# Attention scores in an encoder trunk: the second pass of each head on 128 rows instead of 64, and keys and values in small rings

## The chip, the cores and the metric

The kernel runs on one core of a Trainium2 chip. The metric is the time of one execution on the device in microseconds, the median of several runs. The profile is of one execution; its times are counted from the first instruction.

Five engines work side by side, each through its own instructions in order: TensorE (PE in the profile, with its weight loads as PEld), VectorE (DVE), ScalarE (ACT), GpSimd (POOL) and SyncE (SP), whose queue here issues DMAs. POOL's queue issues others. A matmul needs its stationary operand loaded (LDWEIGHTS) before the moving operand streams through, and its result lands in a bank of PSUM.

## The reference

Two layers over a sequence of 2048 positions of width 1024. Layer 0 runs windowed attention (8 query heads on 2 key/value heads of 64, blocks of 128 positions, each block seeing itself and its two neighbours, with a sink logit), chunked spatial gating and a gate path; layer 1 is a convolution with gated linear scans in both directions. Each ends in a projection and a layer norm. The change touches only the scores of the attention:

```python
kb, vb = band(k), band(v)          # three neighbouring blocks of 128
s = jnp.einsum('bnqhgd,bnkhd->bnhgqk', qb, kb) * (HEAD_DIM ** -0.5)
s = jnp.where(valid, s, NEG_INF)   # |i - j| <= 128
m = jnp.maximum(s.max(-1, keepdims=True), sink_l)
p = jnp.exp(s - m)
o = einsum(p / (p.sum(-1) + exp(sink_l - m)), vb)
```

## The kernel before, in words

All of it is float32. Products that need more than TensorE's fast float32 form gives are made of pieces: a value is split into a high part, rounded to that form, and a low part, the rest, and a product is summed from several passes (`mm3`, lines 151 to 154, has three).

Layer 0 starts with the attention, block by block. For each pair of blocks `build` (line 299) loads x, transposes and modulates it, splits it and stores it. `project(blk)` (line 323) makes q, k and v of one block, rotates q and k on DVE, and prepares the keys: `ks` holds three 128-column pieces, the high part of key head 0 twice side by side, that of key head 1 likewise, and the low parts of both heads. Three transposes (L362) bring them to PSUM, and ACT copies them (L363) into `kT`, one tile for the whole sequence: 128 rows, 3 pieces, 2048 positions. In the first two pieces rows 0 to 63 and rows 64 to 127 hold the same high key part; in the third, rows 0 to 63 hold the low part of head 0 and rows 64 to 127 that of head 1. The values go to `vt`, also one tile for the whole sequence.

`scores(blk)` (line 370) splits q so that of a head's 128 rows one half is the high and the other the low part, transposes it into `qT`, and then makes the scores of each of the 8 heads in two passes into one PSUM bank (`psc`, three buffers):

```python
nc.tensor.matmul(ps[:, 0:W], lhsT=qt[:, h, :], rhs=kT[:, kv, k0:k0 + W], start=True, stop=False)
nc.tensor.matmul(ps[:, 0:W], lhsT=qt[r0:r0 + 64, h, :], rhs=kT[r0:r0 + 64, 2, k0:k0 + W], start=False, stop=True)
```

The first pass (L399) has 128 rows and gives high and low query times high key; the second (L400) has 64 rows and gives high query times low key. The width W is 384, and 256 for the first and the last block. DVE takes the scores out of PSUM with mask and minimum (L402), ACT takes the exponential (L405), DVE divides by the sum (L412). For blocks 0 to 13 DVE then transposes the probabilities in 32x32 squares into the tile `T` (L430; one buffer, two at the end), and 16 DMAs (L437), half of them on SP's queue and half on POOL's (from block 11 on all on SP's), put the squares in place, back into `P` (three buffers). Blocks 14 and 15 are transposed on TensorE (L422). `values(blk)` (line 441) multiplies with the values (L447).

The written order is a loop over blocks: scores of blk + 1, `build` for two blocks at every second, values of blk, projection of blk + 3. A planner, which simulates the program, moves instructions by priority as their inputs come; each engine then keeps the order that the planner gave. Behind the attention's last blocks TensorE already runs the first matmuls of the next stage (`sv_ps`, line 516).

Of the kernel before, what the change touches and what calls it, by code (L numbers as in the profile page):

```python
# [16 lines left out]
S = 2048  # L17
# [36 lines left out]
def kernel(  # L54
# [144 lines left out]
        else:  # L199
            tt(out=dst, in0=ps[pr, 0:w], in1=bias, op=ALU.add)  # L200

# [1 line left out]
    sa = ctx.enter_context(ExitStack())  # L203
    sb = ExitStack()
    ap = pool(sb, "attn", right)
# [83 lines left out]
    nc.gpsimd.affine_select(out=mask, in_=mask, pattern=[[-1, 384]], compare_op=ALU.is_ge, fill=-BIG,  # L289
                            base=256, channel_multiplier=1)  # L290

    kT = ap.tile([128, 3, S], F32R, name="kT")
    vt = ap.tile([128, S // 128, 128], F32, name="vt")
    NB = S // 128
    qkb = {}
    hTs = {}
# [26 lines left out]
    def project(blk):  # L323
        if blk >= NB:
            return
        hT = hTs[blk // 2]
        sl = slice(blk % 2 * 128, blk % 2 * 128 + 128)
        pk = bank(pj, "pj")
        for k in range(KD):
            mm3(pk[:, 0:256], hT[0][k][:, sl], hT[1][k][:, sl], wqh[:, k, 512:768], wql[:, k, 512:768], k == 0,  # L330
                k == KD - 1)
        pq = bank(pj, "pj")
        for k in range(KD):
            mm3(pq, hT[0][k][:, sl], hT[1][k][:, sl], wqh[:, k, 0:512], wql[:, k, 0:512], k == 0, k == KD - 1)
        qk = ap.tile([128, 10, 64], F32, tag="qk", bufs=4, name="qk")
        qkb[blk] = qk
        act(out=qk[:, 8:10, :], in_=pk[:, 0:128].rearrange("p (h d) -> p h d", h=2), func=AF.Copy)
        act(out=vt[:, blk, :], in_=pk[:, 128:256], func=AF.Copy)
        act(out=qk[:, 0:8, :], in_=pq.rearrange("p (h d) -> p h d", h=8), func=AF.Copy)
        rot = ap.tile([128, 4, 10, 8], F32, tag="rot", bufs=2, name="rot")  # L340
        for h0, h1 in ((8, 10), (0, 8)):
            n = h1 - h0
            cb = cos_t[:, blk:blk + 1, :].to_broadcast([128, n, 8])
            sb_ = sin_t[:, blk:blk + 1, :].to_broadcast([128, n, 8])
            t1 = qk[:, h0:h1, 0:8]
            t2 = qk[:, h0:h1, 8:16]
            r0, r1, r2, r3 = (rot[:, i, h0:h1, :] for i in range(4))
            tt(out=r0, in0=t1, in1=cb, op=ALU.mult)
            tt(out=r1, in0=t2, in1=sb_, op=ALU.mult)
            tt(out=r2, in0=t2, in1=cb, op=ALU.mult)  # L350
            tt(out=r3, in0=t1, in1=sb_, op=ALU.mult)
            tt(out=t1, in0=r0, in1=r1, op=ALU.subtract)
            tt(out=t2, in0=r2, in1=r3, op=ALU.add)
        ks = ap.tile([128, 3, 128], F32R, tag="ks", bufs=2, name="ks")
        kf = qk[:, 8:10, :]
        kd = ks[:, 0:2, :].rearrange("p k (u d) -> p k u d", u=2)
        act(out=kd, in_=kf[:, :, None, :].to_broadcast([128, 2, 2, 64]), func=AF.Copy)
        tt(out=ks[:, 2, :].rearrange("p (k d) -> p k d", k=2), in0=kf, in1=kd[:, :, 0, :].bitcast(F32),
           op=ALU.subtract)
        ps = bank(px, "px")  # L360
        for i in range(3):
            nc.tensor.transpose(ps[:, i * 128:i * 128 + 128].bitcast(F32R), ks[:, i, :], ident_r)  # L362
        act(out=kT[:, :, blk * 128:blk * 128 + 128], in_=ps[:, 0:384].rearrange("p (i n) -> p i n", i=3),  # L363
            func=AF.Copy)

    def window(blk):
        lo_b = max(blk - 1, 0)
# [2 lines left out]
    def scores(blk):  # L370
        if blk >= NB:
            return
        lo_b, nb = window(blk)
        W = nb * 128
        k0 = lo_b * 128
        m0 = (lo_b - blk + 1) * 128
        qk = qkb.pop(blk)
        qs = ap.tile([128, 8, 128], F32R, tag="qs", bufs=1, name="qs")
        qt = ap.tile([128, 8, 128], F32R, tag="qT", bufs=2, name="qT")
        nm = ap.tile([128, 8], F32, tag="nm", bufs=2, name="nm")  # L380
        rs = ap.tile([128, 8], F32, tag="rs", bufs=2, name="rs")
        es = ap.tile([128, 8], F32, tag="es", bufs=2, name="es")
        P = ap.tile([128, 8, 384], F32, tag="P", bufs=3, name="P")
        for kv in range(2):
            hs = slice(4 * kv, 4 * kv + 4)
            qv = qs[:, hs, :].rearrange("p h (u d) -> p h u d", u=2)
            split(qv[:, :, kv, :], qv[:, :, 1 - kv, :], qk[:, hs, :])
            ps = bank(px, "px")
            for i in range(4):
                nc.tensor.transpose(ps[:, i * 128:i * 128 + 128].bitcast(F32R), qs[:, 4 * kv + i, :], ident_r)  # L390
            act(out=qt[:, hs, :], in_=ps.rearrange("p (h n) -> p h n", h=4), func=AF.Copy)
        for kv in range(2):
            hs = slice(4 * kv, 4 * kv + 4)
            p = P[:, hs]
            r0 = 64 * kv
            for g in range(4):
                h = 4 * kv + g
                ps = bank(psc, "psc", (128, 384))
                nc.tensor.matmul(ps[:, 0:W], lhsT=qt[:, h, :], rhs=kT[:, kv, k0:k0 + W], start=True, stop=False)  # L399
                nc.tensor.matmul(ps[:, 0:W], lhsT=qt[r0:r0 + 64, h, :], rhs=kT[r0:r0 + 64, 2, k0:k0 + W],  # L400
                                 start=False, stop=True)
                nc.vector.tensor_tensor_reduce(  # L402
                    out=p[:, g, 0:W], in0=ps[:, 0:W], in1=mask[:, m0:m0 + W], scale=-0.125,
                    scalar=nsink[:, h:h + 1], op0=ALU.add, op1=ALU.min, accum_out=nm[:, h:h + 1])
                act(out=p[:, g, 0:W], in_=p[:, g, 0:W], func=AF.Exp, scale=-1.0, bias=nm[:, h:h + 1],  # L405
                    accum_out=rs[:, h:h + 1])
            tt(out=es[:, hs], in0=nm[:, hs], in1=nsink[:, hs], op=ALU.subtract)
            act(out=es[:, hs], in_=es[:, hs], func=AF.Exp)
            tt(out=rs[:, hs], in0=rs[:, hs], in1=es[:, hs], op=ALU.add)
            nc.vector.reciprocal(rs[:, hs], rs[:, hs])  # L410
            for g in range(4):
                ts(out=p[:, g, 0:W], in0=p[:, g, 0:W], scalar1=rs[:, 4 * kv + g:4 * kv + g + 1], scalar2=None,  # L412
                   op0=ALU.mult)
        nk = 4 * nb
        T = (tail[-1] if tail and blk % 2 else tq).tile([128, 12, 256], F32, tag="T", bufs=1, name="T")
        if blk >= PE_FROM:
            tv = T.rearrange("p j m -> p (j m)").rearrange("p (j v n) -> p j v n", j=3, v=2)
            for kv in range(2):
                for j in range(nb):
                    ps = bank(psc, "psc")  # L420
                    for g in range(4):
                        nc.tensor.transpose(ps[:, g * 128:g * 128 + 128], P[:, 4 * kv + g, j * 128:j * 128 + 128], ident)  # L422
                    if j % 2:
                        nc.vector.tensor_copy(tv[:, j, kv], ps)
                    else:
                        act(out=tv[:, j, kv], in_=ps, func=AF.Copy)
            Pb[blk] = tv
            return
        for kv in range(2):
            nc.vector.transpose(  # L430
                out=T[:, 0:nk, 128 * kv:128 * kv + 128].rearrange("p j (g q) -> p g j q", q=32),
                in_=P[:, 4 * kv:4 * kv + 4, 0:W].rearrange("p g (j q) -> p g j q", q=32))
        pv = P.rearrange("p h c -> p (h c)").rearrange("p (j i m) -> p j i m", j=3, i=4)
        for i in range(4):
            for r in range(4):
                dma = nc.sync if blk >= 11 or (i + r) % 2 == 0 else nc.gpsimd
                dma.dma_start(out=pv[32 * r:32 * r + 32, 0:nb, i],  # L437
                              in_=T[32 * i:32 * i + 32, 0:nk].rearrange("p (j r) m -> p r j m", r=4)[:, r])
        Pb[blk] = pv

    def values(blk):
# [2 lines left out]
        ops = bank(po, "po")  # L444
        for j in range(nb):
            for kv in range(2):
                nc.tensor.matmul(ops[64 * kv:64 * kv + 64, :], lhsT=vt[:, lo_b + j, 64 * kv:64 * kv + 64],  # L447
                                 rhs=pv[:, j, kv] if blk >= PE_FROM else pv[:, j, :, 128 * kv:128 * kv + 128],
                                 start=(j == 0), stop=(j == nb - 1))
        t, b = divmod(blk, 4)  # L450
# [72 lines left out]
    sb.close()  # L523


# [1 line left out]
    tp = pool(sp, "temp", left)  # L527
    pjb = pool(sp, "pjb", left, bufs=2, space=PSUM)
    pm = pool(sp, "pm", left, bufs=2, space=PSUM)
# [293 lines left out]
            vectors1()  # L823


# [1 line left out]
    sd.close()  # L827
    sp.close()
    turn = None
# [266 lines left out]

    se.close()

# [1 line left out]
    op = pool(ctx, "outp", right)  # L1100
    g_bc = op.tile([128, D], F32, name="g_bc1")
    b_bc = op.tile([128, D], F32, name="b_bc1")
# [74 lines left out]
```

## Time and profile before

| | |
|---|---|
| median of 3 runs | 1629.59 us (1624.6 to 1631.48) |
| span of the profiled execution, which is the only time that the profile gives for it | 1623.0 us |
| PE busy | 1525.7 us, 94% |
| DVE busy | 1243.6 us, 77% |
| ACT busy | 779.7 us, 48% |
| POOL busy | 517.0 us, 32% |
| score passes L399 and L400 | 128 each, from 67.7 to 372.1 us |
| key copies L363 | 16, from 60.2 to 314.3 us, 491 ns each |
| DMA | 366.72 MB, 226 GB/s in the mean |

Busy time is counted from start to modelled end, and matmuls overlap, so the distance from one matmul's start to the next start is what it costs PE. The time of a wait is put down to what ended last before the waiting instruction started; "issue" means that nothing the profile shows ended it.

### The profile page before, as it was taken

What the parts mean: (1) busy time and instruction counts of PE and PEld (TensorE: products, weight loads), DVE (VectorE), ACT (ScalarE), POOL (GpSimd) and SP (SyncE); (2) the same over time, 40 slices, a digit from 0 to 9 for tenths busy, and PEclk for the clock granted to TensorE, in tenths of its full rate; (3) what the DMA queues carried; (4) which work ended last, traced back from release to release, by engine and by line L of the source; (5) the groups of instructions that cost most, each with busy time, mean ns of one, the idle gap of its engine ahead of it and who ended that gap; (6) DMA issues with size and microseconds to landing.
All of it is one profiled execution on the core that took longest, in us unless ns stands there. A gap on an engine that the chain in (4) does not pass through costs nothing. (4 is left out here: it accounts for less than half of the span.)

```text
span 1623.0 us, 21775 instructions
## 1 busy us (share of the span) xinstructions
PE 1525.7 (94%) x7016; PEld 1193.3 (74%) x7016; DVE 1243.6 (77%) x2243; ACT 779.7 (48%) x1448; POOL 517.0 (32%) x703
## 2 busy tenths in 40 slices
PE   3999999999999999999999998999999899979997
PEld 3776666666787877887887776777787787867886
DVE  8478788765678667966776767879979989887795
ACT  3556666544332343243243307488478587771100
POOL 1022223202003200310120344867847765433121
PEclk9899999999999999999999998999999999999999
DMA  9356666765898989888785797787695757559652
GB/s 333 122 150 169 176 182 183 230 185 164 295 272 283 286 266 306 298 281 264 243 299 164 198 267 171 244 208 238 208 240 182 241 188 243 184 193 373 224 199 87
DMA packets 204602, 366.72 MB, mean 226 GB/s; under 512 B 54568, under 2 KB 100804, under 8 KB 204488
## 3 DMA queue, kind: packets, MB, share of 16 engines
q1 hardware_dynamic: 166632, 235.25, 46.8%
q0 software_dynamic: 37856, 130.08, 26.3%
q8 instruction: 56, 0.92, 0.2%
q14 instruction: 58, 0.48, 0.1%
HBM read 264.07 MB, written 79.68 MB: 212 GB/s over the span
## 5 line engine op out<-in xcount | busy, mean ns | idle before, releaser
L152 PE MATMUL pj<-ahi,hl 128*128 128x512 f32 x512 | 202.2, 398 | 10.1 <-DMA hl<-w_d 9.0
L148 ACT ACTIVATE hl<-raw 128x512 fp32r<-128x512 f32 x192 | 118.8, 628 | 192.5 <-DMA raw<-in_ev_w_in_dram 125.6
L153 PE MATMUL pj<-alo,hl 128*128 128x512 f32 x512 | 202.7, 396 | 0.0
L154 PE MATMUL pj<-ahi,hl 128*128 128x512 f32 x512 | 202.1, 396 | 0.0
L149 DVE TENSOR_TENSOR hl<-raw,hl 128x512 fp32r<-128x512 f32 x192 | 131.9, 695 | 66.8 <-ACT hl L148 66.4
L152 PEld LDWEIGHTS pj<-ahi,hl 128*128 128x128 f32 x512 | 97.6, 191 | 33.9 <-DMA hl<-w_d 11.3
L153 PEld LDWEIGHTS pj<-alo,hl 128*128 128x128 f32 x512 | 98.3, 192 | 20.6
L154 PEld LDWEIGHTS pj<-ahi,hl 128*128 128x128 f32 x512 | 97.9, 191 | 21.1
L402 DVE CUSTOM_DVE_ANT_0 P<-psc,mask,nsink 128x384 f32<-128x384 f32 (+1 forms) x128 | 75.6, 597 | 48.1 <-PE psc L400 45.6
L437 POOL DMA_DIRECT2D P<-T x88 | 48.3, 556 | 171.4 <-DMA xp<-in_x_dram 81.3
L853 POOL DMA_DIRECT2D hl<-w_d x128 | 71.0, 557 | 71.7 <-PE pj L154 59.5
L148 ACT ACTIVATE phl<-praw 128x512 fp32r<-128x512 f32 x56 | 35.4, 632 | 115.9 <-DMA praw<-in_od_w_in_dram 59.7
L499 POOL DMA_DIRECT2D ahi<-h_d x16 | 8.9, 558 | 255.5 <-PE px L154 146.6
L152 PE MATMUL pj<-wqh,hhi 128*128 128x256 f32 (+1 forms) x256 | 89.8, 354 | 0.0
L405 ACT ACTIVATE P<-P,nm 128x384 f32<-128x384 f32 (+1 forms) x128 | 76.4, 599 | 26.5 <-DVE nm L402 24.7
L153 PE MATMUL pj<-wql,hhi 128*128 128x256 f32 (+1 forms) x256 | 88.8, 347 | 0.0
L154 PE MATMUL pj<-wqh,hlo 128*128 128x512 f32 (+1 forms) x256 | 85.9, 349 | 0.0
L144 POOL TENSOR_SCALAR rstd<-mv 128x1 f32<-128x1 f32 x32 | 26.7, 834 | 185.8 <-DVE mv L588 160.4
L148 ACT ACTIVATE ahi<-yt 128x512 fp32r<-128x512 f32 (+1 forms) x44 | 32.4, 745 | 106.0 <-DVE yt L1073 67.9
L749 POOL TENSOR_TENSOR alo<-hm,ahi 128x512 fp32r<-128x512 f32 x32 | 47.9, 1498 | 94.7 <-issue 66.2
L919 DVE SCALAR_TENSOR_TENSOR xc<-X,vcol,xc 128x512 f32<-128x512 f32 (+2 forms) x96 | 77.2, 826 | 0.3
L152 PE MATMUL pm<-xhi,hg 128*128 128x512 f32 (+3 forms) x160 | 57.3, 370 | 19.9 <-ACT ra L938 13.2
(297 smaller groups left out, 4507.9 us busy)
## 6 DMA issues: line engine op xcount, KB each, us to landing
hl<-w_d POOLq DMA_DIRECT2D x128, 512.0 KB, 5.7
raw<-in_ev_w_in_dram SPq DMA_DIRECT2D x128, 256.0 KB, 4.0
w_d<-phl SPq DMA_DIRECT2D x40, 512.0 KB, 4.1
aw<-in_ada_w_dram SPq DMA_DIRECT2D x32, 512.0 KB, 5.9
hg<-w_d POOLq DMA_DIRECT2D x32, 512.0 KB, 4.8
P<-T SPq DMA_DIRECT2D x128, 96.0 KB, 3.7
aw<-in_ada_w_dram SPq DMA_DIRECT2D x8, 1024.0 KB, 8.3
xp<-in_x_dram SPq DMA_DIRECT2D x32, 256.0 KB, 3.5
```

What stands on the lines that cost most here:

```text
L144: nc.gpsimd.tensor_scalar(out=dst, in0=src, scalar1=mul, scalar2=EPS, op0=ALU.mult, op1=ALU.add)
L148: act(out=hi, in_=src, func=AF.Copy)
L149: tt(out=lo, in0=src, in1=hi.bitcast(F32), op=ALU.subtract)
L152: nc.tensor.matmul(ps, lhsT=ahi, rhs=bhi, start=first, stop=False)
L153: nc.tensor.matmul(ps, lhsT=ahi, rhs=blo, start=False, stop=False)
L154: nc.tensor.matmul(ps, lhsT=alo, rhs=bhi, start=False, stop=last)
L402: nc.vector.tensor_tensor_reduce(out=p[:, g, 0:W], in0=ps[:, 0:W], in1=mask[:, m0:m0 + W], scale=-0.125, scalar=nsink[:, h:h + 1], op0=ALU ...
L405: act(out=p[:, g, 0:W], in_=p[:, g, 0:W], func=AF.Exp, scale=-1.0, bias=nm[:, h:h + 1], accum_out=rs[:, h:h + 1])
L437: dma.dma_start(out=pv[32 * r:32 * r + 32, 0:nb, i], in_=T[32 * i:32 * i + 32, 0:nk].rearrange("p (j r) m -> p r j m", r=4)[:, r])
L749: nc.gpsimd.tensor_tensor(out=lo[:, j], in0=h, in1=hi[:, j].bitcast(F32), op=ALU.subtract)
L853: nc.gpsimd.dma_start(out=hl, in_=w_d[i])
L919: stt(out=xc[:, w], in0=xt[:, j0 + j:j0 + j + W], scalar=vcol1[:, 8 * j + g:8 * j + g + 1], in1=xc[:, w], op0=ALU.mult, op1=ALU.add)
```

## The change

The low key parts are stored like the high ones: for each key head twice, in rows 0 to 63 and in rows 64 to 127. `ks` and the key tile have four pieces instead of three. The second pass uses all 128 rows, so it gives high and low query times low key; its stationary operand is the same as that of the first pass.

The key tile for the whole sequence gives way to a ring of two buffers with room for six blocks each: four blocks of their own and one neighbour on each side. The key copy writes a block that is a neighbour of the next or the last group of four into both buffers (blocks 3, 4, 7, 8, 11 and 12). The values get a ring of seven tiles of one block each.

```diff
-    kT = ap.tile([128, 3, S], F32R, name="kT")
-    vt = ap.tile([128, S // 128, 128], F32, name="vt")
+    kTs = {}
+
+    def k_place(n, p):
+        if n not in kTs:
+            kTs[n] = ap.tile([128, 4, 768], F32R, tag="kT", bufs=2, name="kT")
+        return kTs[n][:, :, p * 128:p * 128 + 128]
+
+    vts = {}
...
-        act(out=vt[:, blk, :], in_=pk[:, 128:256], func=AF.Copy)
+        vt = ap.tile([128, 128], F32, tag="vt", bufs=7, name="vt")
+        vts[blk] = vt
+        act(out=vt, in_=pk[:, 128:256], func=AF.Copy)
...
-        ks = ap.tile([128, 3, 128], F32R, tag="ks", bufs=2, name="ks")
+        ks = ap.tile([128, 4, 128], F32R, tag="ks", bufs=2, name="ks")
...
-        tt(out=ks[:, 2, :].rearrange("p (k d) -> p k d", k=2), in0=kf, in1=kd[:, :, 0, :].bitcast(F32),
-           op=ALU.subtract)
+        tt(out=ks[:, 2:4, :].rearrange("p k (u d) -> p k u d", u=2),
+           in0=kf[:, :, None, :].to_broadcast([128, 2, 2, 64]), in1=kd.bitcast(F32), op=ALU.subtract)
         ps = bank(px, "px")
-        for i in range(3):
+        for i in range(4):
             nc.tensor.transpose(ps[:, i * 128:i * 128 + 128].bitcast(F32R), ks[:, i, :], ident_r)
-        act(out=kT[:, :, blk * 128:blk * 128 + 128], in_=ps[:, 0:384].rearrange("p (i n) -> p i n", i=3),
-            func=AF.Copy)
+        n, p = divmod(blk, 4)
+        places = [(n, p + 1)]
+        if p == 0 and n > 0:
+            places.insert(0, (n - 1, 5))
+        if p == 3 and blk < NB - 1:
+            places.append((n + 1, 0))
+        for place in places:
+            act(out=k_place(*place), in_=ps.rearrange("p (i n) -> p i n", i=4), func=AF.Copy)
...
-        k0 = lo_b * 128
+        kT = kTs[blk // 4]
+        k0 = (lo_b - 4 * (blk // 4) + 1) * 128
...
-                nc.tensor.matmul(ps[:, 0:W], lhsT=qt[r0:r0 + 64, h, :], rhs=kT[r0:r0 + 64, 2, k0:k0 + W],
-                                 start=False, stop=True)
+                nc.tensor.matmul(ps[:, 0:W], lhsT=qt[:, h, :], rhs=kT[:, 2 + kv, k0:k0 + W], start=False, stop=True)
...
-                nc.tensor.matmul(ops[64 * kv:64 * kv + 64, :], lhsT=vt[:, lo_b + j, 64 * kv:64 * kv + 64],
+                nc.tensor.matmul(ops[64 * kv:64 * kv + 64, :], lhsT=vts[lo_b + j][:, 64 * kv:64 * kv + 64],
```

More of the change, by code (lines that the diff above doesn't have):

```diff
@@ L394, in scores @@
             p = P[:, hs]
-            r0 = 64 * kv
             for g in range(4):
```

## The prediction

> **What bounds the kernel now.** The change touches only the attention of layer 0, so I first read the page for the whole and then that stage alone. The page's first part, and the stage's stretch from a table of stretches (busy time of each engine, then granted clock, DMA share, GB/s):
>
> ```profile
> span 1623.0 us, 21775 instructions
> PE 1525.7 (94%) x7016; PEld 1193.3 (74%) x7016; DVE 1243.6 (77%) x2243; ACT 779.7 (48%) x1448; POOL 517.0 (32%) x703
> ...
> 60.00:80.00 20.00, 20.00 (x112) 16.13 (x111) 6.91 (x37) 10.32 (x28) 0.00 (x0) 1.00 0.01 1
> 75.00:300.00 225.00, 224.54 (x1142) 153.38 (x1141) 177.90 (x591) 145.64 (x409) 55.83 (x98) 1.00 0.62 171
> ```
>
> PE is busy for 224.54 of 225 us at full clock; DVE is next with 177.90, which is 79%. A busy PE can still be badly used, so the waits of that stretch come next (who waited for whom: us in total, times, longest), PE's first and then the five largest of DVE:
>
> ```profile
> PE px L310 <- DMA xp<-in_x_dram: 0.4, 1, 0.4
> ...
> PEld psc L400 <- issue: 20.6, 92, 0.8
> ...
> DVE P L402 <- PE psc L400: 30.4, 26, 3.2
> DVE qs L149 <- ACT qs L148: 7.1, 6, 2.6
> DVE rs L409 <- ACT es L408: 2.6, 3, 1.2
> DVE ks L358 <- ACT ks L357: 1.9, 2, 1.4
> DVE hlo L149 <- ACT hhi L148: 1.9, 3, 0.9
> ```
>
> PE waits for nobody: it sets the pace, and DVE waits for the scores (30.4 us). But the weight load of the 64-row pass L400 sits 20.6 us in "issue", 92 times: something in PE's own stream is slow. The timeline of PE shows it; the first column is the start, and what a pass costs is the distance to the next start:
>
> ```profile
> 216.40 0.33 PE L399 MATMUL psc<-kT,qT 128*128 128x384 f32 x1
> 216.66 0.43 PE L400 MATMUL psc<-kT,qT 64*128 64x384 f32 x1
> 217.02 0.44 PE L399 MATMUL psc<-kT,qT 128*128 128x384 f32 x1
> 217.40 0.43 PE L400 MATMUL psc<-kT,qT 64*128 64x384 f32 x1
> 217.76 0.44 PE L399 MATMUL psc<-kT,qT 128*128 128x384 f32 x1
> 218.13 0.44 PE L400 MATMUL psc<-kT,qT 64*128 64x384 f32 x1
> 218.50 0.39 PE L154 MATMUL pj<-wqh,hlo 128*128 128x256 f32 x1
> 218.73 0.28 PE L152 MATMUL pj<-wqh,hhi 128*128 128x256 f32 x1
> 218.85 0.28 PE L153 MATMUL pj<-wql,hhi 128*128 128x256 f32 x1
> ...
> 219.54 0.39 PE L153 MATMUL pj<-wql,hhi 128*128 128x512 f32 x1
> 219.77 0.39 PE L154 MATMUL pj<-wqh,hlo 128*128 128x512 f32 x1
> ```
>
> Between 128-row matmuls the distance is 0.12 us for 256 columns (218.73 to 218.85) and 0.23 for 512 (219.54 to 219.77): 384 columns should take 0.175 us. Where a 128-row and a 64-row pass alternate, it is 0.36 to 0.38, and the 256-column matmul right behind (218.50) takes 0.23, not 0.12. Each change of the row count costs about 0.19 us.
>
> The Trainium skill (TensorEngine Tiling, Key Properties) says that a change of the tiling mode drains the engine; the trace agrees, with those 0.19 us. Another of its pages (TensorE: Matmul & The Clock Gate, LDWEIGHTS) says that a load's time does not hang on the row count, and by that alone a full-row pass would gain nothing; the pace of the rows above speaks for the drain.
>
> **The change, part by part.** The pace of a block today, from its key copy, of which blocks 2 and 14 are shown, and beside it the rows from which the added work is priced:
>
> ```profile
> 77.49 0.49 ACT L363 ACTIVATE kT<-px 128x384 fp32r<-128x384 f32 x1
> ...
> 308.34 0.49 ACT L363 ACTIVATE kT<-px 128x384 fp32r<-128x384 f32 x1 [1.30 <-PE px L362]
> ...
> L391 ACT ACTIVATE qT<-px 128x512 fp32r<-128x512 f32 x32 | 18.8, 595 | 17.6 <-PE px L390 17.4
> L149 DVE TENSOR_TENSOR qs<-qk,qs 128x256 fp32r<-128x256 f32 x32 | 12.5, 418 | 7.7 <-ACT qs L148 7.7
> L358 DVE TENSOR_TENSOR ks<-qk,ks x16: 277/290/293, 56.4 to 307.1; 128x128 fp32r<-128x128 f32 x16
> 211.91 0.37 PE L362 MATMUL px<-ident_r,ks 128*128 128x128 f32 x3
> 212.12 0.46 PE L152 MATMUL pj<-wqh,hhi 128*128 128x512 f32 x1
> ```
>
> Twelve blocks in 230.85 us: 19.24 us a block.
>
> *The second pass on 128 rows.* Six passes from 216.40 to 218.50 take 2.10 us, 0.70 for a head; at 0.175 a pass it is 0.35, and with the matmul behind a group of heads (0.11 each) I take 0.37 saved for a head. Eight heads in a block: 2.96 us. No 128-row pair of 384 columns stands in the trace, so the bounds are nothing saved (0.37 a pass stays) and 0.40 a head; I take 0.37, by the 256- and 512-column rows on either side.
>
> *Low keys stored twice.* L358 grows from 128x128 to 128x256: from 290 to the 418 ns of the qs row, 0.13 us a block on DVE, 2 us in all, and it stands two blocks ahead of its use. One transpose more for a block: three start in 0.21 us (211.91 to 212.12), so 0.07 us of PE.
>
> *The copies into the key ring.* L363 grows from 491 to the 595 ns of the qT row, and 6 of the 16 blocks (3, 4, 7, 8, 11, 12) write a second place: 16 x 0.10 + 6 x 0.60 = 5.2 us on ACT. ACT is busy 145.64 of 225 us, so at 19.24 us a block it has 6.8 us idle, and that covers a second copy with its 0.6. If that cover were gone, all 5.2 us would count.
>
> *The rings' new waits.* The first write into a reused key buffer (block 7 into that of blocks 0 to 3, block 11 likewise) waits on ACT's queue for the last score pass of block 3, or 7; behind it stand the exponentials L405, and for these wait DVE's sums and PE. In program order that last pass is two blocks ahead, some 34 us, so I take nothing. The bounds are nothing and one block of 19.24 us at each of the two places. A value tile comes round after seven blocks, and its last reader stands three blocks ahead: nothing. The buffers are not larger (a row of kT has 24,576 bytes as before, the values 3,584 where 8,192 were). No DMA is added or moved.
>
> **What is late next.** PE's need falls to 19.24 - 2.96 + 0.07 = 16.35 us a block. DVE: 177.90/225 x 19.24 = 15.21 busy, plus 0.13, plus its waits for ACT (7.1 + 2.6 + 1.9 + 1.9 = 13.5 us in the stretch, 1.15 a block), 16.5 if they all stay. The third is easily missed. The probabilities go through one buffer T: DVE transposes into it (L430), 16 DMAs read it out (L437, half on SP's queue), and only then can the next block's L430 write. For two blocks, DVE's transposes, SP's queue, and the median landing of these DMAs (last column):
>
> ```profile
> 239.74 3.42 DVE L430 STREAM_TRANSPOSE T<-P 128x1536 f32<-128x1536 f32 x2
> 259.05 3.43 DVE L430 STREAM_TRANSPOSE T<-P 128x1536 f32<-128x1536 f32 x2
> 277.67 3.43 DVE L430 STREAM_TRANSPOSE T<-P 128x1536 f32<-128x1536 f32 x2
> ...
> 245.84 0.37 SPq L304 DMA_DIRECT2D xp<-in_x_dram  x1
> 246.56 6.23 SPq L437 DMA_DIRECT2D P<-T  x8
> 262.51 7.88 SPq L437 DMA_DIRECT2D P<-T  x8
> ...
> P<-T SPq DMA_DIRECT2D x8, 96.0 KB, 5.8
> P<-T SPq DMA_DIRECT2D x8, 96.0 KB, 5.1
> ```
>
> For the later block, T is taken from 259.05 to 262.51 + 7.88 + 5.1 = 275.49, or 16.44 us, and the next L430 starts at 277.67. For the earlier one, SP's queue stood behind loads of x until 246.56, and T came free at 246.56 + 6.23 + 5.8 = 258.59, 18.85 us after its start, just before 259.05. So T alone asks for 17.65 us a block on average (estimate from two blocks). Part of the earlier block's delay are loads that wait for PE's transposes, and these come sooner with a faster PE; I take 0.35 off. The new pace is 17.3 us a block, bound by T and by DVE nearly together, and PE will wait about 1 us in each.
>
> **The sum.** Twelve blocks x (19.24 - 17.3) = 23.3. Ahead of 77.49 lie five heads in a stretch where DVE has only 6.91 of 20 us: 5 x 0.37 = 1.9. Behind 308.34 come 25 heads, 9.3 us at most. There each block waits in turn for the transposes and DMAs of the one two before, and PE for data (the gap at 316.44 below), so I take less than half, 4. In all 29 us, so a span of 1594 where the page has 1623.0. The median of the runs shown is 1629.59, their lowest 1624.6, so the profiled execution is a fast one; against the median the forecast is 1600. Nothing behind the attention is tied to absolute time and PE is at 94% over the whole, so I count the gain as kept.
>
> **The rivals.**
> (B) *PE stays the bound.* T and DVE keep up, all 128 heads count: 128 x 0.37 = 47, and 2 in the tail, 1580. For it: DVE's list of waits above has none for T's DMAs. Against: T's margin of 0.46 us (258.59 against 259.05) at today's pace.
> (C) *The shuffle holds.* If most blocks need the 18.85 us, 12 x 0.39 + 1.9 = 6.6 us, 1623; if half as bad, 1614. For it: SP's queue is in order and holds the loads of x. Against: the later block's 16.44.
> (D) *The full-row pass is no faster.* If the 0.37 comes from two passes into one bank and not from the row count, nothing is saved and the 16 transposes add 1.1: 1631. The Trainium skill's sentence on the load (TensorE: Matmul & The Clock Gate, LDWEIGHTS), named above, points this way. Against: the projection's passes share a bank at 0.23 for 512 columns.
> (E) *Slower, by the clock.* Today PE never waits, and its clock stays at 1.00. Where it did wait in the tail, it dropped:
>
> ```profile
> 316.44 1.19 PE L152 MATMUL pja<-hl,ahi 128*128 128x512 f32 x2 [1.39 <-DMA ahi<-h_d]
> 317.43 0.52 PE L399 MATMUL psc<-kT,qT 128*128 128x384 f32 x1
> ...
> 321.60 0.63 PE L152 MATMUL pja<-hl,ahi 128*128 128x512 f32 x1
> ```
>
> From 316.44 to 321.60 stand 6 passes of 0.23 and 2 heads of 0.73, 2.8 us at full clock, in 5.16: such a fall costs 2.3 us. If PE's new waits bunch into one gap of 1.4 us or more in each block, it decides from 29/2.3 = 13 falls on, one a block; two in each of 14 blocks would cost 64 and end at 1664. Against: 1 us of wait a block, in pieces. The Trainium skill (TensorE: Matmul & The Clock Gate, The HAM clock gate) asks for a whole idle window of about 3.4 us before the clock halves; the fall here came behind 1.39, so the trace is the stricter.
>
> **How the numbers follow.** My forecast (T and DVE pace, 1586 to 1614) 0.64; B 0.15; C 0.10; D 0.06; E 0.05. The range reaches from 1578 (B with the 0.40 bound) to 1616 (C's milder half): it leaves out the rest of C, D, E and a tail of B, about 0.2. A measurement here can tell about 0.5% from no change, so faster means below 1621.4. A, B and most of C: 0.88; D and the rest of C: 0.07; slower, E: 0.05.
>
> **What would show it.** L400 has 128 rows and starts 0.175 us behind L399, and its load's "issue" wait is gone; key copies 17.3 us apart; DVE's wait for psc well below 30.4, and new waits of PE for DVE or of L430 for P<-T's DMAs. Wrong if the passes still stand 0.37 apart, if the clock falls below 1.00 between 75 and 300 us, or if L363 waits for a score pass.

## The result, and the profile after

The changed kernel takes 1601.73 us in the median (1597.13 to 1601.9, four runs); the kernel before, run beside it, 1627.09 (1623.1 to 1631.48). The ratio is 0.984, with an interval of 0.982 to 0.986. A second series of the same kernel (e4_after below) gave 1597.85 us and 0.981 (0.977 to 0.984). The change makes the kernel faster by 25 to 29 us in the medians; 1600, or 29 us less, was forecast.

The page's first part after, and the same stretch of the attention as before (busy time of PE, PEld, DVE, ACT and POOL, then granted clock, DMA share, GB/s):

```profile
span 1600.0 us, 21817 instructions
PE 1481.9 (93%) x7032; PEld 1189.1 (74%) x7032; DVE 1241.8 (78%) x2243; ACT 780.8 (49%) x1454; POOL 514.5 (32%) x703
...
75.00:300.00 225.00, 216.13 (x1265) 170.54 (x1264) 197.55 (x660) 164.41 (x462) 62.85 (x108) 0.99 0.71 203
```

In the same 225 us PE now issues 1265 matmuls where it issued 1142, and it is no longer busy throughout: 224.54 became 216.13. DVE rose from 177.90 to 197.55, 88%. The timeline of PE shows why:

```profile
213.82 0.41 PE L413 MATMUL psc<-kT,qT 128*128 128x384 f32 x1
214.07 0.33 PE L414 MATMUL psc<-kT,qT 128*128 128x384 f32 x1
214.24 0.33 PE L413 MATMUL psc<-kT,qT 128*128 128x384 f32 x1
214.41 0.33 PE L414 MATMUL psc<-kT,qT 128*128 128x384 f32 x1
214.59 0.33 PE L413 MATMUL psc<-kT,qT 128*128 128x384 f32 x1
214.76 0.34 PE L414 MATMUL psc<-kT,qT 128*128 128x384 f32 x1
214.94 1.03 PE L316 MATMUL px<-ident,xp 128*128 128x128 f32 x8
```

From 214.07 to 214.94 stand five passes in 0.87 us, 0.174 each; before, a pass took 0.36 to 0.38. The weight loads show where the time was lost. Before, across a change of the row count, a load starts only when its own pass does (these two belong to the passes L400 at 216.66 and L399 at 217.02):

```profile
216.66 0.18 PEld L400 LDWEIGHTS psc<-kT,qT 64*128 64x128 f32 x1 [0.30 <-issue]
217.02 0.19 PEld L399 LDWEIGHTS psc<-kT,qT 128*128 128x128 f32 x1 [0.18 <-issue]
```

After, a load starts together with the pass ahead of its own (these two belong to the passes at 214.24 and 214.41), so its 0.19 us are hidden:

```profile
214.07 0.19 PEld L413 LDWEIGHTS psc<-kT,qT 128*128 128x128 f32 x1
214.24 0.19 PEld L414 LDWEIGHTS psc<-kT,qT 128*128 128x128 f32 x1
```

In the kernel before, all 128 loads of L400 start within 0.03 us of their own pass; after, those of L414 lead it by 0.17 us in the median. The 0.19 us that a change costs is as much as one load that isn't hidden. Whether PE empties itself at the change, or only takes its next load too late, these rows don't separate.

The waits of the stretch 75 to 300 us (who waited for whom: us in total, times, longest):

```profile
DVE P L415 <- PE psc L414: 13.3, 16, 2.2
...
ACT kT L378 <- PE px L370: 5.7, 6, 2.5
...
PE pj L154 <- DVE hlo L149: 3.7, 3, 2.2
...
PE px L316 <- DMA xp<-in_x_dram: 1.9, 2, 1.6
PE pja L152 <- DMA ahi<-h_d: 1.8, 1, 1.8
...
DVE T L443 <- DMA raw<-in_ev_w_in_dram: 0.9, 1, 0.9
...
PEld psc L414 <- issue: 0.8, 1, 0.8
```

The weight load of the second pass, which sat 20.6 us in "issue", has 0.8 left. DVE waits 13.3 us for scores instead of 30.4, and PE has waits of its own, some 9 us in all, for DVE, for x and for the next stage's data. The key copies of blocks 2 and 14 give the pace, and the first matmul of the gating stage (the tile `pjb`; count, shortest, median and longest ns, first and last start) marks the end of the attention:

```profile
75.08 0.59 ACT L378 ACTIVATE kT<-px 128x512 fp32r<-128x512 f32 x1
...
279.68 0.60 ACT L378 ACTIVATE kT<-px 128x512 fp32r<-128x512 f32 x1 [0.67 <-PE px L370]
```

```profile
L152 PE MATMUL pjb<-ahi,hl x128: 387/389/628, 348.1 to 827.5; 128*128 128x512 f32 x128
```

The same row of the kernel before:

```profile
L152 PE MATMUL pjb<-ahi,hl x128: 389/389/510, 379.1 to 857.3; 128*128 128x512 f32 x128
```

A block takes (279.68 - 75.08)/12 = 17.05 us instead of 19.24, and the attention ends 31.0 us sooner, at 348.1. The span fell by only 23.0. The remainder of the span, behind that first matmul, is 1243.9 us before and 1251.9 after. More on those 8 us in the point on the kept gain below.

### The profile page after: what moved, and what is told of

Its sections match the earlier page's. It is cut to its first block, busy times and chain, and to the rows that moved or that the text cites. A ratio compares the mean times of both kernels' runs of the same rounds, so it can differ in the third digit from the quotient of the medians.

```text
span 1600.0 us, 21817 instructions
## 1 busy us (share of the span) xinstructions
PE 1481.9 (93%) x7032; PEld 1189.1 (74%) x7032; DVE 1241.8 (78%) x2243; ACT 780.8 (49%) x1454; POOL 514.5 (32%) x703
## 5 line engine op out<-in xcount | busy, mean ns | idle before, releaser
L149 DVE TENSOR_TENSOR hl<-raw,hl 128x512 fp32r<-128x512 f32 x192 | 132.1, 697 | 70.4 <-ACT hl L148 70.0
L415 DVE CUSTOM_DVE_ANT_0 P<-psc,mask,nsink 128x384 f32<-128x384 f32 (+1 forms) x128 | 73.7, 596 | 20.6 <-PE psc L414 20.0
```

The lines of the kernel that those rows point to most:

```text
L149: tt(out=lo, in0=src, in1=hi.bitcast(F32), op=ALU.subtract)
L415: nc.vector.tensor_tensor_reduce(out=p[:, g, 0:W], in0=ps[:, 0:W], in1=mask[:, m0:m0 + W], scale=-0.125, scalar=nsink[:, h:h + 1], op0=ALU ...
```

## The experiments

The theory: a change of the row count costs PE about 0.19 us each time, and without these changes the pace is set by DVE and the buffer T nearly together. The rivals: the gain comes from the rings or from another order of the planner; or 64 rows are slow as such; or PE is still the bound.

For all runs, with pace by the key copies of blocks 2 to 14, end of the attention by the first `pjb` matmul, and the rest of the span:

| run | ratio to before (interval) | us a block | attention ends | rest |
|---|---|---|---|---|
| before; again (e5_before) | | 19.24; 19.27 | 379.1; 378.8 | 1243.9; 1247.6 |
| after; again (e4_after) | 0.984 (0.982 to 0.986); 0.981 (0.977 to 0.984) | 17.05; 17.18 | 348.1; 350.2 | 1251.9; 1248.4 |
| e1_ring: rings alone | 1.003 (1.001 to 1.005) | 19.36 | 379.3 | 1255.6 |
| e8_64rows: second pass back on 64 rows | 1.006 (1.004 to 1.009) | 19.51 | 379.6 | 1251.6 |
| e10_all64: both passes on 64 rows | 0.995 (0.993 to 0.998) | 18.18 | 361.6 | 1252.6 |
| e3_grouped | 1.000 (0.998 to 1.002) | 19.25 | 377.7 | 1253.5 |
| e6_forced | 1.004 (1.002 to 1.006) | 19.41 | 384.7 | 1245.8 |
| e7_nodiv | 0.997 (0.995 to 1.000) | 18.81 | 369.6 | 1252.8 |
| e9_xpool | 0.988 (0.986 to 0.990) | 16.64 | 352.5 | 1250.4 |
| e12_split | 0.982 (0.978 to 0.987) | 17.06 | 350.3 | 1244.8 |
| e13_both | 0.987 (0.984 to 0.990) | 16.62 | 354.0 | 1253.5 |
| e11b_xpool_mid | 0.986 (0.983 to 0.989) | 17.05 | 349.0 | 1250.0 |

**The rings without the full-row pass: e1_ring.** The changed kernel with three pieces of keys and the 64-row pass:

```diff
-            kTs[n] = ap.tile([128, 4, 768], F32R, tag="kT", bufs=2, name="kT")
+            kTs[n] = ap.tile([128, 3, 768], F32R, tag="kT", bufs=2, name="kT")
...
-        for i in range(4):
+        for i in range(3):
...
-                nc.tensor.matmul(ps[:, 0:W], lhsT=qt[:, h, :], rhs=kT[:, 2 + kv, k0:k0 + W], start=False, stop=True)
+                nc.tensor.matmul(ps[:, 0:W], lhsT=qt[r0:r0 + 64, h, :], rhs=kT[r0:r0 + 64, 2, k0:k0 + W],
+                                 start=False, stop=True)
```

> The rings alone: keys six blocks at a time and values in a ring of seven, but three key pieces and the 64-row second pass as before. If the gain comes from the row count (my theory), this kernel is as before, within 0.5%: passes 0.36 to 0.38 us apart, key copies 19.2 us apart, span about 1623 to 1626 us (6 copies of 0.49 us more on ACT, hidden). If the rings carry part of the gain (rival: other buffers let the planner start work earlier), key copies come below 18.5 us apart and the span below 1615. If the extra copies cost something, up to 3 us more.

It took 1632.41 us, and its attention ends where that of before does (379.3 against 379.1): the rings bring nothing there. Over the whole the kernel is even 5.4 us slower than the one before in the same series (1626.99), more than the 3 us allowed for; this lies behind the attention (see the last part of the point-by-point section).

**One line back: e8_64rows.** The changed kernel, with everything stored twice and copied twice as it is, and only the second pass on 64 rows again:

```diff
-                nc.tensor.matmul(ps[:, 0:W], lhsT=qt[:, h, :], rhs=kT[:, 2 + kv, k0:k0 + W], start=False, stop=True)
+                nc.tensor.matmul(ps[:, 0:W], lhsT=qt[64 * kv:64 * kv + 64, h, :], rhs=kT[64 * kv:64 * kv + 64, 2 + kv, k0:k0 + W], start=False, stop=True)
```

> The changed kernel with one line back: the second pass takes only the 64 rows of its key head, as before; tiles, rings, copies and the order of every engine's instructions are those of the changed kernel. If the row count carries the gain (theory), passes stand 0.37 us apart again, key copies about 19.2 us, attention over at 376 to 380 instead of 349, and the time is back at 1625 to 1632. If the planner's other order carries part of it (rival: the two kernels with reordered passes showed that order alone can cost 20 us), the time stays below 1615.

Its instructions stand on every engine in the same order as the changed kernel's, so the row count is the only difference. It took 1635.07 us (1624.68 for the kernel before in the same series), 33 us more than the first series of the changed kernel and 37 more than the second, and 3 more than the expected range. Its timeline of PE:

```profile
235.18 0.41 PE L413 MATMUL psc<-kT,qT 128*128 128x384 f32 x1
235.52 0.44 PE L414 MATMUL psc<-kT,qT 64*128 64x384 f32 x1
235.89 0.44 PE L413 MATMUL psc<-kT,qT 128*128 128x384 f32 x1
```

And its waits between 75 and 300 us:

```profile
DVE P L415 <- PE psc L414: 27.3, 26, 3.9
PEld psc L414 <- issue: 20.1, 93, 0.3
```

The distance of 0.34 to 0.37 is back, and the 20.1 us of "issue" with it; the attention ends at 379.6. So the whole gain hangs on the row count of this one line. The larger key copies and their second places are all in this kernel too, and its attention ends only 0.5 us later than that of before.

**64 rows, or the change of rows: e10_all64.** Both passes on the same 64 rows. The first pass leaves out the low query part, so less is computed; the written order of the instructions is again the changed kernel's.

```diff
-                nc.tensor.matmul(ps[:, 0:W], lhsT=qt[:, h, :], rhs=kT[:, kv, k0:k0 + W], start=True, stop=False)
-                nc.tensor.matmul(ps[:, 0:W], lhsT=qt[:, h, :], rhs=kT[:, 2 + kv, k0:k0 + W], start=False, stop=True)
+                nc.tensor.matmul(ps[:, 0:W], lhsT=qt[64 * kv:64 * kv + 64, h, :], rhs=kT[64 * kv:64 * kv + 64, kv, k0:k0 + W], start=True, stop=False)
+                nc.tensor.matmul(ps[:, 0:W], lhsT=qt[64 * kv:64 * kv + 64, h, :], rhs=kT[64 * kv:64 * kv + 64, 2 + kv, k0:k0 + W], start=False, stop=True)
```

> The changed kernel with both passes on the same 64 rows (the first pass leaves out the low part of the query, so that term is missing), in the same order of instructions. If the change of the row count is what costs (theory), a pass behind a pass takes 0.175 us though it has 64 rows, and only the ends of a run of passes cost, about 0.09 us in front and 0.11 behind: a head between projections about 0.55 us, in a run of heads 0.35; attention over at 355 to 362 and the time 1604 to 1612. If a 64-row pass is slow by itself (rival), each takes 0.36 and the time is as with the 64-row second pass or worse, 1625 or more.

The timeline of PE in this run:

```profile
137.07 0.39 PE L154 MATMUL pj<-wqh,hlo 128*128 128x512 f32 x1
137.39 0.45 PE L413 MATMUL psc<-kT,qT 64*128 64x384 f32 x2
137.67 0.34 PE L414 MATMUL psc<-kT,qT 64*128 64x384 f32 x2
137.85 0.33 PE L413 MATMUL psc<-kT,qT 64*128 64x384 f32 x1
138.02 0.34 PE L414 MATMUL psc<-kT,qT 64*128 64x384 f32 x1
138.29 0.39 PE L152 MATMUL pj<-wqh,hhi 128*128 128x256 f32 x1
138.51 0.28 PE L153 MATMUL pj<-wql,hhi 128*128 128x256 f32 x1
...
224.15 0.44 PE L413 MATMUL psc<-kT,qT 64*128 64x384 f32 x1
224.43 0.33 PE L414 MATMUL psc<-kT,qT 64*128 64x384 f32 x1
224.61 0.33 PE L413 MATMUL psc<-kT,qT 64*128 64x384 f32 x1
...
225.13 0.34 PE L414 MATMUL psc<-kT,qT 64*128 64x384 f32 x1
225.39 0.88 PE L316 MATMUL px<-ident,xp 128*128 128x128 f32 x6
```

Between two 64-row passes the distance is 0.17 to 0.18 us, the same as between two 128-row passes. So 64 rows aren't slow; the change is, going in and coming out, and its price falls half on the matmul ahead of it and half on the one behind. Going in, the projection at 137.07 takes 0.32 instead of 0.23, and the first passes behind it 0.28 instead of 0.17 (132.36 to 132.53 in the changed kernel). Coming out, the last pass takes 0.27 (138.02 to 138.29) and the projection behind it 0.22 instead of 0.12. Behind transposes the first pass proves less: it takes 0.28 here (224.15 to 224.43), but 0.25 in the changed kernel too (213.82 to 214.07), where the row count doesn't change. Before, every 64-row pass had a change on both of its sides; here only a group's two ends have one. The time follows: 1616.0 us, 19 less than e8_64rows, where the changed kernel is 33 to 37 below it. The attention ends within the expected range, the time lies 4 us above it.

One thing besides the change of rows is in this run. The two passes at 137.39 start 0.006 us apart, and so do, within 0.01 us, the two at 137.67: they are the last head of one key head, on rows 0 to 63, and the first of the other, on rows 64 to 127, side by side. This happens in 7 of the 16 blocks and saves some 0.35 us each time (an estimate, two passes of 0.175), 2.5 us in all, so it does not carry the result. The Trainium skill (TensorE: Matmul & The Clock Gate, Why this matters for your kernels) says that a single matmul over few rows takes the time of one over 128, and the distances of 0.17 to 0.18 agree. It also says that a change of the tiling mode drains the engine (TensorEngine Tiling, Key Properties), and the two ends of a group agree, as they would with a load that comes too late.

**The same saving in the kernel before: e3_grouped and e6_forced.** The passes of two heads in the order 128, 128, 64, 64, which halves the changes of row count without any other storage. First in program order only:

```diff
+                if g % 2 == 0:
+                    for j in (h, h + 1):
+                        pss[j] = bank(psc, "psc", (128, 384))
+                        nc.tensor.matmul(pss[j][:, 0:W], lhsT=qt[:, j, :], rhs=kT[:, kv, k0:k0 + W], start=True,
+                                         stop=False)
+                    for j in (h, h + 1):
+                        nc.tensor.matmul(pss[j][:, 0:W], lhsT=qt[r0:r0 + 64, j, :],
+                                         rhs=kT[r0:r0 + 64, 2, k0:k0 + W], start=False, stop=True)
```

> The kernel before, with its three key pieces and whole-sequence tiles, but the passes of two heads are ordered 128, 128, 64, 64 rows: half as many changes of the row count, the same matmuls. If each change costs about 0.19 us (theory), the second of two like passes starts 0.175 us behind the first, a pair of heads takes about 1.08 us instead of 1.46, and 8 heads save 1.5 us a block: key copies about 17.8 us apart, span about 1623 - 15 = 1608. If a 64-row pass is slow by itself (rival), 64 follows 64 at 0.36 and the gain is at most half of that, span 1616 or more; if two passes into one bank were the cost, both kinds fall to 0.175, 1 a block would be left of the gain, and the first rows of the timeline show it. DVE may get its scores two at a time and give some of it back.

The planner put most passes back in turns, so nothing changed (ratio 1.000). e6_forced adds an ordering edge from the second 128-row pass to the first 64-row one, and then the groups stay:

```diff
+                        if j == h:
+                            tc.add_manual_dep(m2.ins, m1.ins.name,
+                                              mybir.DependencyInfo(mybir.DependencyClass.NoSync,
+                                                                   mybir.DependencyReason.DATA),
+                                              reason="pass order")
```

> The kernel before with the passes of two heads bound to the order 128, 128, 64, 64 rows (in the run before, the planner had mostly put them back into turns). Where two like passes did stand together, the second of them cost 0.175 to 0.18 us and the change between them 0.26 to 0.37. If the change of the row count is the cost (theory), a pair of heads takes 1.0 us instead of 1.46, 8 heads save 1.8 us a block, key copies 17.4 to 17.8 us apart, attention over at about 357 and the span about 1603 to 1608. If the 64-row pass itself is slow (rival), 64 behind 64 takes 0.36 and half of the gain is missing, span 1615 or more. If it lies in the pair of passes into one bank, each pass into another bank than the last takes 0.175 and all four do, attention over near 350.

The passes became cheap where grouped. The timeline of PE in e6_forced:

```profile
216.44 0.51 PE L402 MATMUL psc<-kT,qT 128*128 128x384 f32 x2
216.88 0.61 PE L405 MATMUL psc<-kT,qT 64*128 64x384 f32 x2
217.42 0.44 PE L402 MATMUL psc<-kT,qT 128*128 128x384 f32 x1
```

That is 0.98 us for two heads instead of 1.4. Yet the kernel took 1631.77 us. In the planner's new order PE runs into waits that before did not have, and around some of them the clock fell. The stretch of the attention and a short one inside it, and PE's timeline at the same place:

```profile
75.00:300.00 225.00, 215.44 (x1131) 153.51 (x1131) 171.88 (x591) 144.88 (x407) 56.01 (x98) 0.95 0.61 170
...
200.00:203.00 3.00, 3.00 (x10) 1.30 (x11) 2.77 (x6) 2.11 (x6) 0.00 (x0) 0.50 0.92 311
```

```profile
197.32 1.94 PE L310 MATMUL px<-ident,xp 128*128 128x128 f32 x8 [2.82 <-ACT hhi L148]
...
202.02 4.89 PE L458 MATMUL po<-P,vt 128*64 128x512 f32 x12
```

PE waits 2.82 us for ACT's split, from 194.50 to 197.32, and from 196 us on, in the middle of the wait, the granted clock is 0.50: the twelve value matmuls take 4.89 us where they take 2.79 at full clock. Only from 207 us on is it 1.00 again. This is rival E of the prediction, in another kernel. Over the 225 us PE stood idle for 9.6 us (0.5 before), and its clock was 0.95 in the mean; the changed kernel's is 0.99. The idle time and 0.05 of 225 us for the clock make up to some 20 us (an estimate), about as much as the order was expected to save, 1.8 us a block.

**What bounds the new pace: e7_nodiv.** The changed kernel without the division by the sum (L425), 8 x 0.42 us less on DVE in each block; the output is left unnormalised.

```diff
-            for g in range(4):
-                ts(out=p[:, g, 0:W], in0=p[:, g, 0:W], scalar1=rs[:, 4 * kv + g:4 * kv + g + 1], scalar2=None,
-                   op0=ALU.mult)
```

> The changed kernel without the division by the sum (left out: 8 x 0.42 us of DVE for each block, so the output is not normalised). After the change key copies are 17.05 us apart where PE's stream needs about 16.35. If DVE is what holds PE up (theory), DVE falls from 15.2 to 11.8 us a block and key copies come 16.4 us apart: attention over at about 340 instead of 349, time 8 us lower. If the shuffle buffer T is the hold (rival), it stays within 2 us of the changed kernel. If PE alone is the bound, likewise nothing.

It was not faster than the changed kernel but 19 us slower, at 1620.92. DVE's busy time in the stretch fell to 148.76 us, but in the planned order loads of x stand on SP's queue behind the shuffle's transfers (eight transfers from 148.69 to 157.11, loads of x at 157.21), and PE waited for them (waits of e7_nodiv, 75 to 300 us):

```profile
PE px L316 <- DMA xp<-in_x_dram: 18.6, 5, 5.3
```

The clock was 0.95 in the mean of the stretch. So this run does not tell DVE from T. It shows that another planned order can cost some 20 us here although work is saved.

**The loads of x off SP's queue: e9_xpool.** From the third pair of blocks on, POOL's queue issues them:

```diff
+            ld = load if u < 2 else nc.gpsimd.dma_start
```

> The changed kernel with the loads of x from the third pair of blocks on issued by POOL's queue and not by SP's, where they and the 8 shuffle DMAs of a block wait for each other in order. If that queue costs PE its last microsecond a block (theory), key copies come 16.5 us apart and the time falls by up to 6 us, to about 1594. If PE's waits come from DVE and ACT (rival), the time stays within 2 us of 1600, or rises where the planner's order changes.

The key copies of blocks 2 and 14 now stand (274.88 - 75.15)/12 = 16.64 us a block apart, near PE's own need of 16.35. Yet the kernel took 1605.31 us, and the attention ends at 352.5, later than the changed kernel's. The 16.64 hangs on its last copy alone. Block 13's key copy, in this run and then in the changed kernel:

```profile
261.50 0.60 ACT L379 ACTIVATE kT<-px 128x512 fp32r<-128x512 f32 x1 [0.35 <-PE px L371]
```

```profile
261.42 0.60 ACT L378 ACTIVATE kT<-px 128x512 fp32r<-128x512 f32 x1
```

Up to there both kernels need 16.94 us a block; then block 14's keys come 4.8 us sooner here, and block 15's do not (285.95 against 285.52). So the loads' new queue did not make the front faster; one block's projection moved ahead. The rear of the pipeline, the value products L460 (L461 here) of blocks 1 and 9, stand at 113.61 and 251.26 in the changed kernel, 17.2 us a block, and at 114.39 and 250.66 in this one, 17.0; at block 10 the rear is behind (276.82 against 273.27). From 280 to 350 us ACT and DVE then wait for T's transfers:

```profile
ACT T L440 <- DMA P<-T: 8.8, 1, 8.8
...
DVE T L438 <- DMA P<-T: 6.5, 1, 6.5
DVE T L444 <- DMA P<-T: 4.9, 1, 4.9
```

The changed kernel has the same three waits there, with 7.7, 5.9 and 1.5 us.

**The tail: e12_split, e13_both, e11b_xpool_mid.** From block 11 on, all 16 transfers of a shuffle are issued by SP. In the changed kernel these issues take 11.67 and 10.61 us for the last two blocks. e12_split gives half of them back to POOL for these two; e13_both does the same on top of e9_xpool.

```diff
-                dma = nc.sync if blk >= 11 or (i + r) % 2 == 0 else nc.gpsimd
+                dma = nc.sync if blk == 11 or (i + r) % 2 == 0 else nc.gpsimd
```

> The changed kernel with the value-shuffle transfers of blocks 12 and 13 issued again from two queues, SP and POOL; only block 11 keeps all sixteen on SP. Theory: the end of the attention is set by the chain through tile T, and sixteen issues on SP take 10.6 us there against some 8 us with two queues, so each of two blocks saves about 2.5 us: the last score stretch (block-14 key copy to first pjb matmul) falls from 68.4 to about 64 us, the time to about 1597 us, pace of the blocks unchanged at 17.1. Rival: the tail is set by the projection work and PE, not by T; then the stretch stays within 1 us of 68.4 and the time within 2 us of the changed kernel's.

> The kernel of e9_xpool (x loads of blocks 2 on issued by POOL) with the same split of the shuffle transfers of blocks 12 and 13. Theory: the steady pace stays at 16.6 us a block, and the tail, 77.6 us in e9_xpool with DVE waiting 4.9 us and ACT 8.8 us for T, loses about 5 us: attention ends near 347 us, time about 1600 us. Rival: what e9_xpool lost in its tail comes from PE reaching the tail earlier and T's chain being as long anyhow; then the tail stays above 75 us and the time at about 1605 us.

SP's queue in e12_split, for these two blocks, and DVE's transposes ahead of the second:

```profile
295.27 7.28 SPq L450 DMA_DIRECT2D P<-T  x8
315.90 7.95 SPq L450 DMA_DIRECT2D P<-T  x8
```

```profile
312.39 3.44 DVE L443 STREAM_TRANSPOSE T<-P 128x1536 f32<-128x1536 f32 x2 [0.18 <-issue]
```

The issues are shorter as expected, but the second block's transposes stand at 312.39 where the changed kernel has them at 309.18 (310.87 in e4_after). There they had waited 1.52 us for T's transfers. Here no such wait stands before them; instead DVE had just done three splits of the gating stage's data (L149 at 309.79 and 310.91, behind waits of 1.49 and 0.43 us for ACT). So what was saved on the queue did not bring the transposes forward. The tail from the key copy of block 14 is 350.3 - 279.25 = 71.0 us, longer than 68.4 (69.6 in e4_after), and the time is 1598.86 us, between the two series of the changed kernel. The theory of the queue's issue time fell; so did its half in e13_both, with a tail of 354.0 - 275.29 = 78.7 us and 1607.32 us. For e11b_xpool_mid only the pairs 2 to 5 load x by POOL:

```diff
-            ld = load if u < 2 else nc.gpsimd.dma_start
+            ld = nc.gpsimd.dma_start if 1 < u < 6 else load
```

> The changed kernel with the x loads of the middle four builds (u from 2 to 5, blocks 4 to 11) issued by POOL, and those of the last two again by SP; the shuffle transfers as in the changed kernel. Theory: what e9_xpool and e13_both lost behind the key copy of block 14 (77.6 and 78.7 us where the changed kernel took 68.4) came from the late x loads in POOL's queue, so here the early blocks keep the pace of 16.6 us, the tail returns to about 69 us, the attention ends near 343 us and the time is about 1594 us. Rival: PE, DVE and T have a fixed amount of work up to the end of the attention, and a faster start only makes the tail wait; then the attention ends at 348 to 352 us as in all of these variants and the time stays between 1598 and 1606 us.

The attention ended at 349.0 us and the time was 1603.24, as the rival had it. But the key copies came 17.05 us apart, so the faster start that both expected outcomes took for granted did not come about, and the run does not show what one would have been worth. With the second pass on 128 rows the attention ends between 348.1 and 354.0 us in all of these kernels, except e7_nodiv. None of them measurably beats the changed kernel.

## Why the prediction was right, point by point

**The cost of a change of rows: right.** Predicted 0.19 us a change and 0.175 a pass; measured 0.174 a pass, and in e10_all64 about 0.2 a change. Not in the forecast was that a group's first pass behind transposes takes 0.25 in the changed kernel. Rival D (no faster) is excluded by the changed kernel's own rows, two passes into one bank at 0.174, and by e8_64rows; e10_all64 shows that what counts is the change, not the rows.

**The new pace: right in size, with luck in it.** Predicted 17.3 us a block with PE waiting about 1 us in each; measured 17.05 and 17.18, and PE's non-busy time is (225 - 216.13)/225 x 17.05 = 0.67 us a block. PE's own work is then 16.38, where 16.35 was predicted. But the 17.3 was worked out from T, and this half is not borne out: in the stretch the transposes L443 stood waiting for 1.3 us in all, and no wait for the transfers P<-T is among them. Such waits come in the tail, 280 to 350 us: 1.5 us in the changed kernel, 2.1 in e4_after, 4.9 in e9_xpool. DVE, the other half, is busy 197.55 of 225 us, 88%; PE waits 3.7 us for its splits, but 1.9 for x and 1.8 for the next stage's data as well. What sets the 17.05 was not separated, since e7_nodiv ran into x loads. Rival B (PE alone, 16.35 us a block) was reached by no run, as the 16.64 of e9_xpool comes from one copy; rival C, with 18.85 or half as bad, is excluded by the pace.

**The sum, term by term.** The steady stretch: predicted 23.3, measured 230.85 - 204.60 = 26.25. The head: predicted 1.9, measured 77.49 - 75.08 = 2.4; the trace has six heads there and not five, which makes 2.2 of the prediction's term. The tail: predicted 4, measured (379.1 - 308.34) - (348.1 - 279.68) = 2.3. In all 29 predicted; 31.0 in the first pair of profiles and 28.6 in the second (e5_before and e4_after). The steady term was 3 us too small in the first pair, the tail nearly 2 too large, so the errors partly cancel.

**What was costed at nothing.** The larger key copies (598 ns in the median, 22 of them) are hidden: ACT waited 5.7 us for PE ahead of them, and never for a score pass, so the rings' new wait cost nothing.

**Rival E, the clock: its sign came, its price did not.** The prediction named a clock below 1.00 between 75 and 300 us as a sign of being wrong. It is 0.99 there in both profiles of the changed kernel: one fall to 0.50 for 3.4 us in each, from 287.5 us in the first and from 258.7 in e4_after, which costs 1.7 us at most. E's price needed one fall a block. Its condition, a gap of 1.4 us or more, does not hold either. In the first profile PE waits 2.20 us ahead of 258.35, and the clock stays at 1.00; in e4_after the same wait, 2.21 us ahead of 257.74, is followed by the fall. And in the prediction's own row the clock was down from 315.3 us on, when PE had waited for 0.25 of its 1.39 us. e6_forced shows that such falls can cost much; what sets them off is not shown.

**"I count the gain as kept": the weak step.** In the first pair of profiles 8 of the 31 us were lost behind the attention. The waits of PE there, for the gating stage's output copies, before (380 to 980 us), and then after (350 to 957):

```profile
PE pja L152 <- ACT yt L706: 1.4, 1, 1.4
```

```profile
PE pja L152 <- ACT yt L719: 7.3, 4, 2.6
```

That looks like a new wait made by the change, but it is not one: the second profile of the kernel before has 5.8 us of it and a rest of 1247.6, the second one of the changed kernel has none and a rest of 1248.4. Two executions of one program differ by 3.5 to 3.7 us in the rest, and over the fourteen profiles it lies between 1243.9 and 1255.6 in kernels with and without rings (1253.5 in e3_grouped without, 1244.8 in e12_split with them). The second pair, 1247.6 against 1248.4, gives back 0.8 us. The medians came out at 1601.73 and 1597.85, 25.4 and 29.1 us below the kernel before beside them, so the step held in the second series and nearly in the first. What stays open is why e1_ring and e8_64rows, whose attention ends where that of before does, are 0.3% and 0.6% slower in their medians: in their profiles the difference lies in the rest (1255.6 and 1251.6). It is idle time of PE, which is busy there for 1180 us in both, as in the kernel before (1179 and 1177), and no single wait carries it. Nor does the clock: behind 380 us it stood at 0.50 for 57.2 and 58.1 us in these two, and for 60.5 and 53.9 in the two profiles of the kernel before.

## What to carry to other kernels

Look at the distance between starts of consecutive matmuls, not at their busy time: a PE that is busy for 99.8% of a stretch lost 0.19 us at every change of its row count, and the sign of it was the "issue" wait of the weight load. Where few-row passes stand between full ones, padding them to all rows cost PE only one more transpose a block here. Keeping equal row counts together makes the passes cheap as well, but in e6_forced the new order cost as much as it saved. And do not read a pipeline's pace from its two ends alone: in e9_xpool one block's copy, moved ahead by 4.8 us, made 16.94 us a block look like 16.64.

## What the hardware showed that was not expected

- A pass over 64 rows behind another over the same 64 rows goes at the full rate, 0.17 to 0.18 us for 384 columns, where alternating passes take 0.36 to 0.38 each. Each change costs about 0.2 us, half of it on the matmul ahead and half on the one behind (e10_all64), and across it the weight load starts with its own pass and not with the one ahead.
- Two 64-row passes on different halves of the rows ran side by side: in e10_all64 they started within 0.01 us of each other in 7 of the 16 blocks, where the last head of one key head stood next to the first of the other.
- In e6_forced the granted clock fell to 0.50 some 1.5 us into a wait of PE of 2.82 us, and twelve value matmuls took 4.89 us instead of 2.79; it lasted some 10 us. The Trainium skill (TensorE: Matmul & The Clock Gate, The HAM clock gate) names a whole idle window of about 3.4 us for such a fall; here less was enough, and a wait of 2.20 us in the changed kernel was followed by none.
- The rest of the span behind the attention differs by 3.5 to 3.7 us between two executions of one program, which is as much as several of the effects looked for here. A single pair of profiles cannot settle whether a gain is kept.
